# Strassen sums of the feed-forward's up weights with one operand copied into PSUM by ScalarE, and the eight gate rows two beside each of four column tiles

## The chip, the cores and the metric

The kernel runs on one NeuronCore of a Trainium2 chip. The metric is the device time of one launch in microseconds. The engines are named as the profile names them: PE is the matrix engine (its weight loads stand apart as PEld), DVE the vector engine, ACT the scalar engine, POOL GpSimd, SP the queue that issues all DMAs here. Each engine works through its instructions in the order in which they stand in the program; they wait for each other through semaphores.

## The reference, cut to what matters

One layer of a streaming encoder over 64 sample frames and 512 prompt frames, 576 columns in all, width 1024, all in float32. Attention, convolution and the first gate come first; the change lies in the second half:

```python
h2 = _rmsnorm(x, norm2_g) * (1 + sc2) + sh2
gate, up = jnp.split(h2 @ w_ffn_up, 2, axis=-1)      # w_ffn_up: 1024 x 5632, D_FF = 2816
x = x + gt2 * ((jax.nn.silu(gate) * up) @ w_ffn_down)  # w_ffn_down: 2816 x 1024
```

`gt2` is one of six vectors `silu(c) @ w_ada + b_ada`, one row of 1024 products for each of its 1024 elements and each of the two request groups.

## The kernel before

Activations lie transposed, 128 features on the partitions and tokens along the row. A weight tile is 128 by 128, a chunk is eight of them (512 KB), and every float32 product is made of three float32r matmuls: high part of the weights by high part of the activations, high by low, low by high (`mm3`, lines 323 to 325). So every chunk that arrives in a buffer `wraw` is split in units of four tiles: ACT casts the high part (`whi`, line 297), POOL or DVE subtracts it from the source (`wlo`, line 300). Four buffers of `whi` and four of `wlo` go round, five of `wraw`.

The feed-forward runs in three stretches of column tiles, `FCH`: pairs 0 to 7, 8 to 15, 16 to 21. A pair is one tile of gate columns and one of up columns; its two chunks are called g and u here. In each stretch `up(i)` makes every pair's activations, then `down` multiplies them by eight column tiles of `w_dn`. The up product of a pair is done by a 2 by 2 block scheme with seven products instead of eight, on half the tokens (288 columns) each, of 12 matmuls each. Product m takes as its weights: 1 and 2 the halves g0 and g1 of chunk g, 4 the half u1 of chunk u, and 5, 6, 7, 3 sums of the four halves. For pairs 0 to 7 the products 1 and 2 are made earlier. `pair_source` makes the sums:

```python
two = bank2(("cva", "sa")[n_sum[1] % 2])...      # a two-bank PSUM tile
sums[c, 5], sums[c, 6] = two[:, 0], two[:, 1]
nc.vector.tensor_add(out=sums[c, 5], in0=u0, in1=u1)            # line 270
nc.vector.tensor_sub(out=sums[c, 6], in0=sums[c, 5], in1=g0)    # line 271
```

The sums of one pair are made about one pair ahead of their use, into `cva` and `sa` in turn. Only the first pair's go elsewhere. Line 274 (POOL) makes the sum of product 7, line 277 (DVE) that of product 3.

The products of a pair accumulate in four PSUM banks. In `up`, product 5 goes to a bank `c5`, DVE reads it into `v` (line 1379), and only then may product 3 accumulate on the same bank; product 7 goes to `c7`, DVE adds it (line 1381), and only then may product 4 accumulate there. Line 1376 makes `u`, which 1379 and 1381 need ahead; lines 1383, 1387 and `act` (1372 to 1374) finish the pair.

Beside the first stretch's `down` the vector `gt2` is made, a column tile of it beside each of the eight column tiles of `w_dn`: `gate_row(n)` loads a chunk of `w_ada_n` into a buffer `wraw` (line 1245) and DVE multiplies it with two broadcast rows and sums (line 416, twice; the rows lie in `cva` and `sa`, where `gate_start` puts them). The following pairs' chunks use the same five buffers, and the following pairs' sums use the same two PSUM tiles.

A scheduler fixes each engine's order when the program is built, from the dependencies and its own times; the feed-forward isn't ordered by hand.

Of the kernel before, what the change touches and what calls it, by code (L numbers as in the profile page):

```python
# [87 lines left out]
def layer_kernel(ctx: ExitStack, tc: tile.TileContext, a):  # L88
    nc = tc.nc
# [4 lines left out]
    def sb(shape, tag, dt=F32, bufs=1):  # L94
        return cp.tile(shape, dt, tag=tag, name=tag, bufs=bufs)

    def bank(tag):
        return ps.tile([P, 512], F32, tag=tag, name=tag)

    def bank2(tag):  # L100
        return ps.tile([P, 2, 512], F32, tag=tag, name=tag)
# [83 lines left out]
    def vcol(o, i):  # L185
        return vec[:, o + i : o + i + 1]
# [65 lines left out]
    sums = {}  # L252

    def pair_source(c, m):

        if m in (1, 2):
            return raws[c - 1][:, 4 * m - 4 : 4 * m]
        if m == 4:
            return raws[c][:, 4:8]
        g0, g1, u0, u1 = (raws[c - 1 + x // 2][:, 4 * (x % 2) : 4 * (x % 2) + 4] for x in range(4))  # L260
        if m == 6:

            n_sum[1] += 1
            if n_sum[1] == 1:
                sums[c, 5] = pair_sum()
                sums[c, 6] = bank("m0").rearrange("p (k n) -> p k n", n=P)
            else:
                two = bank2(("cva", "sa")[n_sum[1] % 2]).rearrange("p x (k n) -> p x k n", n=P)
                sums[c, 5], sums[c, 6] = two[:, 0], two[:, 1]
            nc.vector.tensor_add(out=sums[c, 5], in0=u0, in1=u1)  # L270
            nc.vector.tensor_sub(out=sums[c, 6], in0=sums[c, 5], in1=g0)
        elif m == 7:
            sums[c, 7] = pair_sum()
            nc.gpsimd.tensor_sub(out=sums[c, 7], in0=g0, in1=u0)
        elif m == 3:
            sums[c, 3] = pair_sum()
            nc.vector.tensor_sub(out=sums[c, 3], in0=g1, in1=sums[c, 6])
        return sums[c, m]

    n_sum = [0, 0]  # L280

    def pair_sum():
        n_sum[0] += 1
        return ft([P, 4, P], f"wx{n_sum[0] % 2}")
# [44 lines left out]
    def mmbank():  # L329
        l = mmtags["l"]  # L330
        mmtags["i"] += 1
        return bank(l[mmtags["i"] % len(l)])
# [15 lines left out]
    with tc.tile_pool(name="sp", bufs=1) as sp:  # L348
# [153 lines left out]
        with tc.manual_schedule(engines={ENG.PE, ENG.DVE, ENG.Activation, ENG.Pool}):  # L502
            nc.scalar.activation(out=ct, in_=vec[:, V_CT : V_CT + 16].rearrange("p (k g) -> p k g", g=2), func=AF.Silu)
            nc.vector.scalar_tensor_tensor(
                out=bsn, in0=vec[:, V_BA + SC1 : V_BA + SC1 + 8], scalar=1.0, in1=vec[:, V_N1 : V_N1 + 8],
# [64 lines left out]
            for k in range(KT):  # L570
                n = k + 1
# [109 lines left out]
    def pool_tap(i, j):  # L681
# [24 lines left out]
        out=rbd.rearrange("h (q r) -> h q r", r=255),  # L706
        in_=rbs.unsqueeze(1).to_broadcast([16, 64, 255]),
# [18 lines left out]
    def products(kind, i, h):  # L726

        b = gemm(("in", N_IN.index((kind, i))), hx, (h,))[0]

        def out():  # L730
            if kind == "g":
                evac_g(h, b)
            elif kind == "a":
                evac_a(i, h, b)
            elif kind == "k":
                evac_k(i, h, b)
            elif kind == "v":
                evac_v(i, h, b)
            elif kind == "q":
                evac_q(i, h, b)  # L740
            else:
                j = i // 2 if kind == "ga" else gbs(i)
                if h == 0 and i % 2 == 0 and (kind == "ga" or i >= N_EARLY):
                    sigs[j] = sb([P, 2, NT], f"kv{j}")
                c0, c1 = HALF[h]
                o = sigs[j][:, i % 2, c0:c1] if j in sigs else None
                if kind == "gb" and i < N_EARLY:
                    if h == 0:
                        gbr[i] = sb([P, YW], f"gbr{i}") if i < 3 else at([P, NT], "sv")
                    nc.scalar.copy(out=gbr[i][:, c0:c1], in_=b)  # L750
                elif kind == "ga":
                    nc.scalar.copy(out=o, in_=b)
                else:
                    nc.scalar.activation(out=o, in_=b, func=AF.Sigmoid)

        return out
# [216 lines left out]
    with tc.manual_schedule(engines={ENG.PE, ENG.DVE, ENG.Activation, ENG.Pool}):  # L973
        for j, (p, ch, u) in enumerate(steps):
# [7 lines left out]
            out = products(*job[:2], *job[2]) if job else None  # L982
# [32 lines left out]
    with tc.tile_pool(name="lp", bufs=1) as lp:  # L1015
        def lt(shape, tag, dt=F32, bufs=1):
# [5 lines left out]
                            in_=cdram.rearrange("g d -> (g d)").partition_broadcast(P))  # L1022
# [5 lines left out]
        def wide(o):  # L1028
            return vec[:, o : o + 8].unsqueeze(2).to_broadcast([P, 8, 2])
# [110 lines left out]
    def ft(shape, tag, dt=F32, bufs=1):  # L1140
        if tag.startswith("gbr"):
            return sb(shape, tag, dt)
        return fp.tile(shape, dt, tag=tag, name=tag, bufs=bufs)
# [98 lines left out]
    def late_row(j, f, cbt):  # L1242

        t = sb([P, KT, P], "wraw", bufs=RAW).rearrange("p k n -> p (k n)")
        nc.sync.dma_start(out=t, in_=a["w_ada_n"][j])
        dump = sb([P, D], "lsum", BF16)
        ada_cols(ada[:, f], t, cbt, [dump, dump])

    for n in range(8):
# [7 lines left out]
        out=sc_a[:, 1], in0=ada[:, SC2 : SC2 + 8], scalar=1.0, in1=wide(V_N2), op0=ALU.add, op1=ALU.mult  # L1257
# [36 lines left out]
    with tc.manual_schedule(engines={ENG.PE}):  # L1294
# [8 lines left out]
        for j2 in (0, 2):  # L1303
# [6 lines left out]
            for j in t1:  # L1310
                nc.vector.scalar_tensor_tensor(
                    out=t1[j], in0=t1[j], scalar=sh2(j), in1=b0[:, j], op0=ALU.add, op1=ALU.subtract
                )
            for j in t1:
                nc.vector.scalar_tensor_tensor(
                    out=t2[j], in0=x11[:, j], scalar=sh2(4 + j), in1=t1[j], op0=ALU.add, op1=ALU.subtract
# [14 lines left out]
    def gate_start():  # L1331
        for g in range(2):
            cb3[g] = sb([P, KT, P], "wraw", bufs=RAW).rearrange("p k n -> p (k n)")
            nc.sync.dma_start(out=cb3[g], in_=cdram[g].partition_broadcast(P))
            to_psum(cb3, g, ("cva", "sa")[g])

    def gate_row(k):
        late_row(KT + len(ROW_SH) + 24 + k, GT2 + k, cb3)
        nc.vector.tensor_scalar_add(out=ada[:, GT2 + k], in0=ada[:, GT2 + k], scalar1=vcol(V_BA, GT2 + k))
# [63 lines left out]
    for c in range(len(FCH) - 1):  # L1403
        for i in range(*FCH[c]):
            up(i)
        mmtags["i"] = 3
        if c == 0:
            yt = [ft([P, 8, HB], "b0"), *(sb([P, 4, HB], f"kv{6 + x}") for x in range(2))]
            ysum = [[yt[0][:, n] for n in range(8)], [yt[1 + n // 4][:, n % 4] for n in range(8)]]
            gate_start()  # L1410
        for n in range(8):
            if c == 0:
                gate_row(n)
            for h in range(2):
                b = mmbank()[:, :HB]
                down(b, n, c, h)
                if c == 0:
                    nc.scalar.copy(out=ysum[h][n], in_=b)
                else:
                    nc.vector.tensor_add(out=ysum[h][n], in0=b, in1=ysum[h][n])  # L1420
                    residual(n, h, ysum[h][n], GT2)
    c = len(FCH) - 1
# [16 lines left out]
    for n in range(7):  # L1439
# [7 lines left out]
        if n == 1:  # L1447
            r = rst[0][2]()
            for k in range(8):
                nc.vector.scalar_tensor_tensor(  # L1450
                    out=x1[k][:, :HB], in0=x1[k][:, :HB], scalar=vcol(V_NF, k), in1=r, op0=ALU.mult, op1=ALU.mult,
# [5 lines left out]
    with tc.manual_schedule(engines={ENG.PE, ENG.DVE, ENG.Activation, ENG.Pool}):  # L1457
# [10 lines left out]
        for k in (0, 1, 2, 3, 4, 7):  # L1468
            nc.vector.scalar_tensor_tensor(
                out=y[:, k], in0=x1[k][:, HB:], scalar=vcol(V_NF, k), in1=r, op0=ALU.mult, op1=ALU.mult,  # L1470
# [119 lines left out]
```

## Time and profile before

| | us |
|---|---|
| median of three runs (948.9 to 953.95) | 952.08 |
| the profiled execution | 950.14 |
| its span, first to last instruction | 948.4 |
| PE busy in the span | 915.4 |
| DVE busy | 689.8 |
| ACT busy | 465.6 |
| POOL busy | 530.5 |

The profile is of one execution. Times of rows count from the start of its span; 1.74 us lie outside it. The feed-forward's up stretches lie at about 557 to 626 us, 678 to 767 us and 829 to 897 us of the span, its down stretches between and after them.

### The profile page before, as it was taken

How to read it: one execution, taken by the hardware profiler on the slowest of the kernel's cores; microseconds unless marked ns; L12 is line 12 of the kernel's file. 1: busy time of each engine (PE TensorE's matmuls, PEld its weight loads, DVE VectorE, ACT ScalarE, POOL GpSimd, SP SyncE). 2: the span in 40 equal slices, each digit the busy share in tenths (PEclk: the TensorE clock that was granted, in tenths of full speed). 3: DMA queues.
4: the chain of work that ended last, by engine and by line, in shares of the span. 5: the costliest groups of instructions: out<-in, count | busy, mean ns of one | idle time of the engine just before them, and what ended most of it. 6: DMA issues, size and time to landing. Idle time of an engine off the chain costs nothing.

```text
span 948.4 us, 18132 instructions
## 1 busy us (share of the span) xinstructions
PE 915.4 (97%) x6804; PEld 901.8 (95%) x6804; DVE 689.8 (73%) x1372; ACT 465.6 (49%) x1055; POOL 530.5 (56%) x495
## 2 busy tenths in 40 slices
PE   7989999999999999999999999999999999999995
PEld 4989999999999999999999989999899999999995
DVE  6988999868888884589967698844566644556475
ACT  5436555466555566552434764453254541255462
POOL 2759999445454546453573565654367664376322
PEclk8999999999999999999999999999999999999997
DMA  9914423222122123286463244355322232222352
GB/s 338 360 55 53 150 77 100 68 84 68 45 68 68 46 95 106 84 305 224 180 241 112 67 134 134 112 156 198 136 90 90 89 112 72 67 96 88 88 149 100
DMA packets 37918, 116.33 MB, mean 123 GB/s; under 512 B 4243, under 2 KB 9011, under 8 KB 37685
## 3 DMA queue, kind: packets, MB, share of 16 engines
q1 hardware_dynamic: 37830, 115.18, 37.0%
q8 instruction: 53, 0.87, 0.4%
q14 instruction: 35, 0.29, 0.1%
HBM read 111.11 MB, written 4.18 MB: 122 GB/s over the span
## 4 chain that ended last, share of the span: by engine, by line
PE 66%; DVE 16%; DMA 10%; issue 4%; ACT 1%; POOL 1%; SPq 0%; DVEq 0%; ACTq 0%; POOLq 0%
PE m L323 12%; PE m L324 11%; PE m L325 11%; PE s L323 8%; PE s L325 8%; PE s L324 8%; DVE dump L416 5%; DMA wraw<-w_ada_n 3%; DMA wraw<-w_up 3%; DVE lsum L416 2%; DMA wat<-w_ada_n 2%; PE sa L923 1%; DVE h L481 1%; DVE qa L439 1%; DVE wlo L300 1%
## 5 line engine op out<-in xcount | busy, mean ns | idle before, releaser
L300 POOL TENSOR_TENSOR wlo<-wraw,whi 128x512 fp32r<-128x512 f32 x216 | 291.8, 1359 | 217.2 <-ACT whi L297 173.6
L297 ACT CAST whi<-wraw 128x512 fp32r<-128x512 f32 x248 | 149.5, 608 | 162.3 <-PE s L324 86.3
L323 PE MATMUL m<-h,whi 128*128 128x320 f32 (+2 forms) x768 | 227.0, 296 | 2.1 <-ACT whi L297 2.1
L324 PE MATMUL m<-h,whi 128*128 128x320 f32 (+2 forms) x768 | 225.8, 295 | 0.0
L325 PE MATMUL m<-h,wlo 128*128 128x256 f32 (+2 forms) x768 | 225.0, 295 | 0.2 <-DVE wlo L300 0.2
L323 PEld LDWEIGHTS m<-h,whi 128*128 128x128 f32 x768 | 145.1, 189 | 2.8 <-ACT whi L297 2.6
L325 PEld LDWEIGHTS m<-h,wlo 128*128 128x128 f32 x768 | 144.6, 189 | 0.4 <-DVE wlo L300 0.4
L324 PEld LDWEIGHTS m<-h,whi 128*128 128x128 f32 x768 | 144.8, 189 | 0.0
L671 DVE SCALAR_TENSOR_TENSOR cva<-z,vec,cva 128x606 f32<-128x606 f32 x150 | 127.5, 850 | 1.5
L323 PE MATMUL s<-h,whi 128*128 128x288 f32 (+2 forms) x336 | 99.4, 296 | 2.2 <-ACT kv L1287 1.9
L325 PE MATMUL s<-h,wlo 128*128 128x288 f32 (+2 forms) x336 | 98.9, 294 | 0.0
L324 PE MATMUL s<-h,whi 128*128 128x288 f32 (+2 forms) x336 | 98.8, 294 | 0.0
L300 POOL TENSOR_TENSOR wlo<-wx,whi 128x512 fp32r<-128x512 f32 x44 | 56.7, 1291 | 58.3 <-ACT whi L297 52.8
L324 PE MATMUL m<-qa,whi 128*128 128x288 f32 (+2 forms) x272 | 80.3, 295 | 0.0
L323 PE MATMUL m<-qa,whi 128*128 128x288 f32 (+2 forms) x272 | 80.2, 296 | 0.0
L325 PE MATMUL m<-qa,wlo 128*128 128x288 f32 (+2 forms) x272 | 79.9, 294 | 0.0
L323 PE MATMUL s<-qa,whi 128*128 128x288 f32 (+2 forms) x240 | 70.9, 296 | 0.0
L324 PE MATMUL s<-qa,whi 128*128 128x288 f32 (+2 forms) x240 | 70.9, 295 | 0.0
L325 PE MATMUL s<-qa,wlo 128*128 128x288 f32 (+2 forms) x240 | 70.4, 295 | 0.2 <-DVE wlo L300 0.2
L323 PE MATMUL s<-kv,whi 128*128 128x288 f32 x216 | 64.7, 300 | 4.5 <-DVE t L1379 3.5
L323 PEld LDWEIGHTS s<-h,whi 128*128 128x128 f32 x336 | 63.5, 189 | 2.8 <-ACT kv L1287 2.1
L324 PE MATMUL s<-kv,whi 128*128 128x288 f32 x216 | 63.9, 296 | 0.0
(421 smaller groups left out, 2332.5 us busy)
## 6 DMA issues: line engine op xcount, KB each, us to landing
wraw<-w_up SPq DMA_DIRECT2D x52, 512.0 KB, 3.3
wraw<-w_in SPq DMA_DIRECT2D x39, 512.0 KB, 3.4
wat<-w_ada_n SPq DMA_DIRECT2D x16, 512.0 KB, 3.5
wraw<-w_ada_n SPq DMA_DIRECT2D x16, 512.0 KB, 4.1
wraw<-w_dn SPq DMA_DIRECT2D x16, 512.0 KB, 3.5
wraw<-w_dn SPq DMA_DIRECT2D x16, 384.0 KB, 3.1
wraw<-w_ao SPq DMA_DIRECT2D x8, 512.0 KB, 3.4
wraw<-w_co SPq DMA_DIRECT2D x8, 512.0 KB, 4.2
```

The source lines that it names most:

```text
L297: nc.scalar.copy(out=hi, in_=src)
L300: eng.tensor_sub(out=lo, in0=src, in1=hi.bitcast(F32))
L323: nc.tensor.matmul(out, lhsT=hi, rhs=xh, start=first, stop=False, skip_group_check=again)
L324: nc.tensor.matmul(out, lhsT=hi, rhs=xl, start=False, stop=False, skip_group_check=again)
L325: nc.tensor.matmul(out, lhsT=lo, rhs=xh, start=False, stop=last, skip_group_check=again)
L416: nc.vector.scalar_tensor_tensor(out=dumps[g], in0=wt, scalar=1.0, in1=cbt[g], op0=ALU.mult, op1=ALU.mult, accum_out=out[:, g : g + 1],)
L439: nc.vector.scalar_tensor_tensor(out=xt[k][:, s0:s1], in0=xt[k][:, s0:s1], scalar=sc_a[:, 0, k, g : g + 1], in1=rstd[:, s0:s1], op0=ALU.mu ...
L481: nc.vector.scalar_tensor_tensor(out=hl[k][:, s0:s1], in0=xt[k][:, s0:s1], scalar=ada[:, f, g : g + 1], in1=hh[k][:, s0:s1].bitcast(F32), ...
L671: nc.vector.scalar_tensor_tensor(out=acc, in0=src, scalar=w, in1=acc, op0=ALU.mult, op1=ALU.add)
L923: nc.tensor.transpose(pts[0][:, j, u], probs[u][:, j].rearrange("p a b -> p (a b)"), ident)
```

## The change

Two edits. In `pair_source`, ACT copies u0 into the PSUM tile and DVE adds u1 to it there, where DVE added u0 and u1 out of SBUF; the first pair's sum is left as it was. In the first stretch's `down`, column tiles 0 to 3 have two gate rows each, and 4 to 7 none.

```diff
                 two = bank2(("cva", "sa")[n_sum[1] % 2]).rearrange("p x (k n) -> p x k n", n=P)
                 sums[c, 5], sums[c, 6] = two[:, 0], two[:, 1]
-            nc.vector.tensor_add(out=sums[c, 5], in0=u0, in1=u1)
+                nc.scalar.copy(out=sums[c, 5], in_=u0)
+            nc.vector.tensor_add(out=sums[c, 5], in0=sums[c, 5] if n_sum[1] > 1 else u0, in1=u1)
             nc.vector.tensor_sub(out=sums[c, 6], in0=sums[c, 5], in1=g0)
...
         for n in range(8):
-            if c == 0:
-                gate_row(n)
+            if c == 0 and n < 4:
+                gate_row(2 * n)
+                gate_row(2 * n + 1)
             for h in range(2):
```

Lines 270 to 1412 of before stand one line lower in the changed file, those after the second edit two; the new copy is line 270 there, the add 271.

The scheduler also moves instructions. In the second stretch's up pairs, DVE before, where `t<-m` is line 1376, `cva<-wraw` the add, `t<-s` first line 1379 and then 1381:

```order
L1376 TENSOR_TENSOR t<-m_8598,t 128x288
L270 TENSOR_TENSOR cva<-wraw 128x512
L1379 TENSOR_TENSOR t<-s_8599,t 128x288
L271 TENSOR_TENSOR cva<-cva,wraw 128x512
L1381 TENSOR_TENSOR t<-s_8600,t 128x288
L300 TENSOR_TENSOR wlo<-sa,whi 128x512
```

The same place now:

```order
L1377 TENSOR_TENSOR t<-m_8607,t 128x288
L1380 TENSOR_TENSOR t<-s_8608,t 128x288
L271 TENSOR_TENSOR cva<-cva,wraw 128x512
L272 TENSOR_TENSOR cva<-cva,wraw 128x512
L1382 TENSOR_TENSOR t<-s_8609,t 128x288
L301 TENSOR_TENSOR wlo<-sa,whi 128x512
```

The read of product 5 (now line 1380) stands ahead of the add, and the add and the subtraction stand together ahead of the read of product 7 (now 1382). It is so in all pairs of the second and third stretch that make a sum, but for the first of each. On ACT the new copy stands there between two casts of weights, as the third row of this piece of the changed program shows (`m` and `s` are banks of products, `wx` a sum of weights):

```order
L1361 COPY t<-m_8612 128x288
L1374 CAST qa_8518<-s_8462 128x288
L298 CAST whi<-wx_8666 128x512
L298 CAST whi<-wraw 128x512
L270 COPY cva<-wraw 128x512
L298 CAST whi<-wraw 128x512
L1364 ACTIVATE t<-m_8612 128x288
L298 CAST whi<-sa 128x512
```

Behind it stand the next pair's first cast, the silu of product 2 and the cast of the next pair's product 6.

In the first stretch's up pairs the third one's DVE rows before, from the add on (`t<-m` is 1379, then 1381):

```order
L270 TENSOR_TENSOR sa<-wraw 128x512
L1379 TENSOR_TENSOR t<-m_7254,kv_6637 128x288
L300 TENSOR_TENSOR wlo<-cva,whi 128x512
L271 TENSOR_TENSOR sa<-sa,wraw 128x512
L1374 TENSOR_TENSOR qa_7059<-s_7148,qa_7058 128x288
L1381 TENSOR_TENSOR t<-m_7255,t 128x288
```

And now:

```order
L271 TENSOR_TENSOR sa<-sa,wraw 128x512
L1380 TENSOR_TENSOR t<-m_7256,kv_6637 128x288
L301 TENSOR_TENSOR wlo<-cva,whi 128x512
L272 TENSOR_TENSOR sa<-sa,wraw 128x512
L1375 TENSOR_TENSOR qa_7059<-s_7149,qa_7058 128x288
L1382 TENSOR_TENSOR t<-m_7257,t 128x288
```

Here the add stays ahead of the read of product 5, in this pair and in the fifth; in the fourth and the sixth the read comes first.

In the first `down`, SP's queue before, from the two broadcast rows (`cdram`) on; `w_dn` are the down weights, `w_ada_n` the gate rows, `w_up` the next pairs' chunks:

```order
L1334 DMA wraw<-cdram 128x1024 x2
L1245 DMA wraw<-w_ada_n 128x1024
L248 DMA wraw<-w_dn 128x1024
L1245 DMA wraw<-w_ada_n 128x1024
L248 DMA wraw<-w_dn 128x1024
L1245 DMA wraw<-w_ada_n 128x1024
L248 DMA wraw<-w_dn 128x1024
L1245 DMA wraw<-w_ada_n 128x1024
L248 DMA wraw<-w_up 128x1024
L1245 DMA wraw<-w_ada_n 128x1024
L248 DMA wraw<-w_up 128x1024
L1245 DMA wraw<-w_ada_n 128x1024
```

And now:

```order
L1335 DMA wraw<-cdram 128x1024 x2
L1246 DMA wraw<-w_ada_n 128x1024 x2
L248 DMA wraw<-w_dn 128x1024
L1246 DMA wraw<-w_ada_n 128x1024 x2
L248 DMA wraw<-w_dn 128x1024
L1246 DMA wraw<-w_ada_n 128x1024 x2
L248 DMA wraw<-w_dn 128x1024
L1246 DMA wraw<-w_ada_n 128x1024 x2
L248 DMA wraw<-w_up 128x1024 x16
```

All eight gate rows stand ahead of the first chunk of the next pairs, where four of them stood between and behind those chunks. On ACT the copies of pairs 8 and 9 now stand among the casts of the last down chunk, ahead of that chunk's first and second half.

## Rows read from the trace of the kernel before

**Rows 1.** The page's first part: busy time of each engine.
```profile
PE 915.4 (97%) x6804; PEld 901.8 (95%) x6804; DVE 689.8 (73%) x1372; ACT 465.6 (49%) x1055; POOL 530.5 (56%) x495
```

**Rows 2.** PE's waits, 557 to 625 us: who waited for whom, us, times, longest.
```profile
PE m L323 <- DVE t L1379: 1.0, 1, 1.0
PE s L323 <- ACT qa L1373: 0.9, 1, 0.9
PE m L323 <- ACT qa L1373: 0.9, 1, 0.9
PE s L323 <- DVE t L1379: 0.5, 1, 0.5
PE m L323 <- ACT whi L297: 0.4, 1, 0.4
```

**Rows 3.** PE's waits, 690 to 900 us.
```profile
PE s L323 <- DVE t L1379: 3.0, 5, 0.9
```

**Rows 4.** PE's waits, 625 to 690 us.
```profile
PE m L323 <- ACT whi L297: 1.7, 1, 1.7
```

**Rows 5.** Groups by line and shape, from 500 us: busy, mean ns, idle before.
```profile
L270 DVE TENSOR_TENSOR cva<-wraw 128x512 f32<-128x512 f32 x11 | 13.4, 1219 | 15.2 <-DMA wraw<-w_up 15.2
...
L270 DVE TENSOR_TENSOR sa<-wraw 128x512 f32<-128x512 f32 x10 | 11.8, 1180 | 13.2 <-DMA wraw<-w_up 13.2
...
L271 DVE TENSOR_TENSOR cva<-cva,wraw 128x512 f32<-128x512 f32 x11 | 7.5, 686 | 0.0
```

**Rows 6.** Timeline of DVE in the second stretch: start, length, in brackets idle before.
```profile
734.97 1.78 DVE L270 TENSOR_TENSOR sa<-wraw 128x512 f32<-128x512 f32 x1 [2.40 <-DMA wraw<-w_up]
736.67 0.44 DVE L1379 TENSOR_TENSOR t<-s,t 128x288 f32<-128x288 f32 x1
```

**Rows 7.** Timeline of PE at that place and in the first `down`.
```profile
673.69 0.29 PE L323 MATMUL s<-qa,whi 128*128 128x288 f32 x1
...
736.11 0.29 PE L325 MATMUL s<-kv,wlo 128*128 128x288 f32 x1
737.26 0.37 PE L323 MATMUL s<-kv,whi 128*128 128x288 f32 x1 [0.85 <-DVE t L1379]
737.47 0.29 PE L324 MATMUL s<-kv,whi 128*128 128x288 f32 x1
...
738.93 0.29 PE L323 MATMUL m<-h,whi 128*128 128x288 f32 x1
```

**Rows 8.** Timeline of DVE in the third stretch, where PE does not wait.
```profile
843.71 0.71 DVE L270 TENSOR_TENSOR cva<-wraw 128x512 f32<-128x512 f32 x1 [2.37 <-DMA wraw<-w_up]
```

**Rows 9.** Timeline of ACT: a copy of 1024 columns into PSUM, three casts.
```profile
635.53 1.02 ACT L172 COPY sa<-wraw 128x1024 f32<-128x1024 f32 x1 [3.44 <-DMA wraw<-cdram]
636.48 0.62 ACT L297 CAST whi<-wraw 128x512 fp32r<-128x512 f32 x1
...
665.84 0.62 ACT L297 CAST whi<-wraw 128x512 fp32r<-128x512 f32 x1 [0.98 <-PE s L324]
...
735.03 0.62 ACT L297 CAST whi<-wraw 128x512 fp32r<-128x512 f32 x1 [1.23 <-PE m L324]
```

**Rows 10.** Timeline of DVE in the first stretch, the third pair.
```profile
579.36 1.56 DVE L270 TENSOR_TENSOR sa<-wraw 128x512 f32<-128x512 f32 x1 [0.49 <-DMA wraw<-w_up]
580.83 0.44 DVE L1379 TENSOR_TENSOR t<-m,kv 128x288 f32<-128x288 f32 x1
```

**Rows 11.** Line 416 from 625 us on: shortest, median, longest ns, first and last start.
```profile
L416 DVE SCALAR_TENSOR_TENSOR lsum<-wraw,cva x8: 1207/1222/1222, 636.8 to 676.2; 128x1024 bf16<-128x1024 f32 x8
```

**Rows 12.** Timeline of DVE after the last gate row.
```profile
678.58 0.70 DVE L270 TENSOR_TENSOR cva<-wraw 128x512 f32<-128x512 f32 x1
```

**Rows 13.** Busy time and instructions by stretch: PE, PEld, DVE, ACT, POOL, clock, DMA.
```profile
679.90:686.05 6.15, 4.23 (x19) 3.77 (x18) 3.73 (x7) 3.12 (x6) 3.39 (x3) 0.72 0.25 84
686.05:692.20 6.15, 6.15 (x49) 6.15 (x48) 2.92 (x5) 2.14 (x4) 4.72 (x4) 1.00 0.40 131
```

**Rows 14.** The page's DMA issues: number, KB each, us to landing.
```profile
wraw<-w_up SPq DMA_DIRECT2D x52, 512.0 KB, 3.3
```

## The prediction

> **What bounds the kernel now.** I read the page's first part first: PE is busy for 915.4 us of the 948.4 us span, no other engine for more than 73% [rows 1]. The change neither adds nor removes a matmul, so whatever it gives or takes comes out of PE's idle time and of stretches at the lower clock. PE's waits by stretch come next. In the first up stretch there are two of 0.9 us on ACT's `qa` (line 1373), one of 1.0 and one of 0.5 on DVE's line 1379, and one of 0.4 on a cast [rows 2]. In the second and third stretch five add up to 3.0 us, all on line 1379 [rows 3]. Where the first `down` passes into pair 8 there is one of 1.7 us on a cast [rows 4]. These are all that the change can reach.
>
> Why line 1379 is late is in DVE's timeline: line 270 waits 2.40 us for a chunk of `w_up`, starts at 734.97, takes 1.78 us, and 1379, queued behind it, starts at 736.67, though it needs nothing of that chunk [rows 6]. PE had started the last matmul of the products ahead at 736.11 and stood 0.85 us until 1379 was through [rows 7]. The eleven sums into `cva` alone waited 15.2 us for their chunks [rows 5].
>
> **What a wait costs.** From 736.11 to the second matmul behind the wait, 737.47, are 1.36 us; two steps at 0.126 us (6.15 us for 49 matmuls, [rows 13]) would take 0.25, so 1.11 is lost against 0.85 of idle time. I add 0.26 to every wait.
>
> **The copy and the add: durations.** A copy by ACT of 1024 columns into PSUM takes 1.02 us, a cast of 512 columns 0.62 [rows 9]. The new copy of 512 columns lies between half of the one, 0.51, and the other, 0.62; I take 0.6, nearer to the row of equal width. 21 copies are 12.6 us on an engine busy for 465.6 us [rows 1].
>
> The add now has one operand in PSUM. The nearest row is line 271, the same operation in that form: 686 ns on the mean of eleven, against 1219 for line 270 [rows 5]. So DVE should spare 0.5 us a time, 11 us in all, nearly none of it on the path. Line 270 is not always long: 0.71 us at 843.71 [rows 8] and 0.70 at 678.58 [rows 12], 1.78 at 734.97 [rows 6]; in the trace it is long where POOL works beside it. The Trainium skill has a rule for this ("SBUF — State Buffer", section Who interferes with whom): a DVE instruction with two inputs in SBUF contends with a GpSimd instruction that reads SBUF, one with a single such input doesn't. Line 271's even 686 ns agree with it, and by it the add takes that time everywhere. If instead the chunk just landed made the operation slow, the add would stay at up to 1.78 us; the shortened waits below would then not shrink, 0.5 us less in the sum. I take 0.69.
>
> **A: the second and third stretch.** There line 1379 (now 1380) stands ahead of the add, and at once follows 1376, long before product 3 needs it. All five waits go: 3.0 + 5 x 0.26 = 4.3 us. What is late next is the read of product 7, line 1381 (now 1382), which now stands behind add and subtraction. For the pair of [rows 6]: landing 734.97, copy 0.6, add 0.69, subtraction 0.69, the read itself 0.44 (as line 1379), end at 737.39. Product 4 starts four matmuls behind 738.93 [rows 7], at 739.43 by the step above; without the wait 1.11 earlier, 738.32. Some 0.9 us of slack, so no new wait. On ACT the copy delays the cast of 735.03 to 735.57, and it is over at 736.2; its weights are used at 738.93 - 1.11 = 737.8 [rows 7, 9]. The silu and the cast of product 6 behind move by about 0.5 us and are due later still. The add is in PSUM, so the chunk's buffer comes free as before: its last reader is a later split or sum, and the transfers keep their distance from PE.
>
> **B: the first stretch.** The two waits of 0.9 stand on ACT's cast `qa`, line 1373, which reads what DVE's line 1372 leaves; I take them for the fourth and sixth pair, where 1372, like 1379, stood behind line 270. Now both come ahead of the add there: 1.8 + 2 x 0.26 = 2.3 us go. In the third and fifth the add stays ahead of the read: before, 1.56 us from 579.36 and 1379 at 580.83 [rows 10]; now copy and add, 0.6 + 0.69 = 1.29, so 0.27 earlier, twice, 0.5 us. The 0.4 us on a cast stays [rows 2]. Together 2.8.
>
> **C: the gate rows.** Before, each row's chunk reuses the buffer of the row ahead: a transfer (3.3 us for such a size, [rows 14]) and two of line 416 (1.22 each) make some 5.8, and the starts measured, 636.8 to 676.2 for eight, are 5.63 apart [rows 11]. The sums of pairs 8 and 9 stand behind the last on DVE, the first at 678.58 [rows 12]; PE, done with `down`, waits 1.7 us [rows 4], and the granted clock of the next 6.15 us is 0.72: a part of them at 1.2 GHz, 19 matmuls against 49 in the 6.15 us behind [rows 13]. Lost: 30 x 0.126 = 3.8 us.
>
> Now two chains run beside each other, four rows long. A round takes at least 5.63, and at most one transfer and four of line 416, 3.3 + 4.9 = 8.2, so the last row ends between 636.8 + 3 x 5.63 + 4.9 = 658.6 and 666.3; I take 662, between them. The pairs' chunks, queued behind on SP, land up to two transfers later: 669, at worst 673. The sums need them by 678.5, so the wait goes and the clock stays up, 3.8 us. What could be late in its place are the casts of the last down chunk, before which the two copies now stand on ACT: the last of these casts ran at 665.84 [rows 9], PE used it at 673.69 [rows 7], and it now comes at 669 + 0.6, hidden by 3 us; at the worst, 673 + 1.2, PE waits a half us there. The down chunk that now queues behind the second row on SP starts 2 to 3 us later, with several column tiles before it is due.
>
> **The sum.** 4.3 + 2.8 + 3.8 = 10.9 us; 950.14 - 10.9 = 939.2 for an execution like the profiled one. That one lies 1.94 below the median of the three runs, so on the median 952.08 - 10.9 = 941.2, which is my number; 939.2 belongs in the range. If smaller gaps of PE beside the listed waits go too, which the rows do not list, the low end is lower; I put it at 937, two us under 939.2.
>
> **The rivals.** (i) *The transition keeps its wait*: the pairs' chunks come as late as before, since SP works in order and a split of `down` holds a buffer. Against it speak the 12 us between 666.3 and 678.5. It gives 941.2 + 3.8 = 945.0. Chance 0.12.
>
> (ii) *The wait moves on*: product 4 waits for 1382 in place of product 3, or ACT's queue, stopped by the copy, delays a cast. For it speaks that ACT did stop 3.44 us for a transfer with a cast behind it [rows 9]. The Trainium skill ("PSUM — Partial Sum Buffer", section Engine vs sequencer instructions) says that ScalarE's queue is strictly first in, first out; by that alone every us that a chunk lands later holds the casts behind the copy as long, and the trace's cast at 636.48 agrees. Half of A and B lost: 941.2 + 3.6 = 944.8. Chance 0.13.
>
> (iii) *No change*: both of these together, because the chunks land late throughout: 10.9 - 3.8 - 3.6 = 3.5 us left, 948.6, which lies within 0.5% (4.8 us). Chance 0.12.
>
> (iv) *Slower*: the order add, subtraction, 1382 makes product 4 wait in every steady pair. Slack is 0.9 us; beyond it each us of landing costs PE one us in some 13 pairs. To lose the 10.9 and 4.8 more, 15.7 / 13 = 1.2 us a pair: decided at landings 2.1 us later than now, out of a transfer of 3.3 [rows 14]. It would need transfers to start later, and nothing in the change holds a buffer longer but the copy's 0.6. It gives 957 or more. Chance 0.08.
>
> **How the numbers follow.** The forecast has 0.55: 937 to 942.5, the costs' bounds and the 1.94 among it. To hold 8 in 10 the range takes in (i) and (ii), 937 to 947. What a measurement can tell from no change is about 0.5%, 4.8 us; faster by more is the forecast with (i) and (ii), 0.80; within it 0.12; slower 0.08.
>
> **What would show it.** In the profile after: lines 271 and 272 both at 0.69 us, the copy at 0.5 to 0.62; no wait of PE on 1380 in the second and third stretch, none on 1382; two short ones left in the first; the last gate row before 667, no wait of PE at the start of pair 8 and a granted clock of 1.00 there. The forecast is wrong if PE waits for 1382 or a `whi` cast in most pairs, if the copies wait longer than DVE's sums did, or if the clock falls anywhere in `down`.

## The result

The changed kernel takes 937.61 us (median of six runs, 935.88 to 938.70), the kernel before 953.02 in its six (947.32 to 956.32): a ratio of 0.985, interval 0.9827 to 0.9873. The forecast was 941.2 with a range of 937 to 947, and faster with a chance of 0.80. In later comparisons the kernel before has medians of 949.86 (23 runs), 950.13 and 948.44 (11 each); against these the gain is 11 to 12.5 us.

The profiled execution of the changed kernel takes 935.88 us, its span is 934.1 against 948.4. The page of it, against [rows 1]:

```profile
PE 909.1 (97%) x6804; PEld 898.9 (96%) x6804; DVE 678.0 (73%) x1372; ACT 476.2 (51%) x1076; POOL 526.1 (56%) x495
```

DVE lost 11.8 us, ACT gained 10.6, POOL lost 4.4. Where the 14.3 us of span are is seen when the start of each matmul, counted from the start of the span, is compared in the two traces:

| part of the program | forecast, us | gained, us |
|---|---|---|
| up to 555 us (557 in the trace before), the same instructions in the same order | 0 | 2.0 |
| B, first up stretch | 2.8 | 3.6 |
| C, passage into pair 8 | 3.8 | 3.9 |
| A, second and third stretch | 4.3 | 4.8 |
| the rest | 0 | 0.0 |

So the change is worth 12.3 us between these two executions, and 2.0 are what executions differ by ahead of it. (The expectations below take 3.5, 4.0 and 4.7 for B, C and A, a tenth off each.) Of the 2.0, 1.0 is one wait that the list in [rows 2] leaves out: PE waited 1.9 us for a copy by ACT (line 1287) just ahead of 557 us in the kernel before, and waits 0.9 us for it now. The first pair's sums, which the change leaves as they were, stand ahead of that copy; their add took 1.78 us in that execution and takes 0.69 in this one.

PE's waits after, 557 to 625 us, against [rows 2] (who waited for whom, us, times, longest); the second stands in the second pair, where the wait of 0.4 us on a cast was:

```profile
PE m L324 <- DVE t L1380: 0.4, 1, 0.4
PE s L324 <- DVE t L1380: 0.2, 1, 0.2
```

From 625 to 690 us there is none, where [rows 4] had 1.7 (and one of 0.2 on a split, not listed there), and from 690 to 900 only this one, on a split, where [rows 3] had 3.0 on the read of product 5:

```profile
PE s L326 <- DVE wlo L301: 0.2, 1, 0.2
```

The sums' groups from 500 us on, against [rows 5] (busy, mean ns, idle before and for whom):

```profile
L271 DVE TENSOR_TENSOR cva<-cva,wraw 128x512 f32<-128x512 f32 x11 | 7.7, 698 | 16.6 <-ACT cva L270 16.5
L272 DVE TENSOR_TENSOR cva<-cva,wraw 128x512 f32<-128x512 f32 x11 | 7.6, 695 | 0.2
...
L270 ACT COPY cva<-wraw 128x512 f32<-128x512 f32 x11 | 6.5, 591 | 11.5 <-DMA wraw<-w_up 11.5
```

Add and subtraction take 0.70 us each, the copy 0.59, in every pair. DVE's wait for the chunk has become one for ACT's copy, about as long (16.6 us against 15.2 for `cva`); what changed is what stands behind it. DVE in a pair of the second stretch:

```profile
722.34 0.46 DVE L1380 TENSOR_TENSOR t<-s,t 128x288 f32<-128x288 f32 x1 [0.91 <-PE s L326]
724.49 0.70 DVE L271 TENSOR_TENSOR sa<-sa,wraw 128x512 f32<-128x512 f32 x1 [1.69 <-ACT sa L270]
725.23 0.70 DVE L272 TENSOR_TENSOR sa<-sa,wraw 128x512 f32<-128x512 f32 x1
725.84 0.45 DVE L1382 TENSOR_TENSOR t<-s,t 128x288 f32<-128x288 f32 x1
```

ACT there, the copy and the cast that it stands ahead of:

```profile
723.87 0.59 ACT L270 COPY sa<-wraw 128x512 f32<-128x512 f32 x1 [0.99 <-DMA wraw<-w_up]
724.40 0.62 ACT L298 CAST whi<-wraw 128x512 fp32r<-128x512 f32 x1
```

And PE's first matmul of product 4 in this pair:

```profile
727.44 0.29 PE L324 MATMUL s<-kv,whi 128*128 128x288 f32 x1
```

The read of product 5 is over at 722.80, long before the add. The read of product 7, behind the subtraction, ends at 726.29, 1.15 us ahead of its use.

At the passage, the gate rows' first multiplication (shortest, median, longest ns, first and last start), against [rows 11]:

```profile
L417 DVE SCALAR_TENSOR_TENSOR lsum<-wraw,cva x8: 1208/1221/1222, 631.0 to 656.1; 128x1024 bf16<-128x1024 f32 x8
```

The two copies for pairs 8 and 9 on ACT:

```profile
659.12 0.59 ACT L270 COPY sa<-wraw 128x512 f32<-128x512 f32 x1 [4.36 <-DMA wraw<-w_up]
...
665.15 0.59 ACT L270 COPY cva<-wraw 128x512 f32<-128x512 f32 x1 [4.59 <-DMA wraw<-w_up]
```

And the stretch that answers to the first of [rows 13] (the columns after the length are PE, PEld, DVE, ACT and POOL busy, each with its count, the granted clock and DMA):

```profile
672.45:678.60 6.15, 6.15 (x49) 6.15 (x48) 1.74 (x3) 3.24 (x7) 4.19 (x4) 1.00 0.29 85
```

Rows that took 39 us from first to last start take 25 [rows 11]; the clock stays at 1.00, and PE runs 49 matmuls where it ran 19.

### The profile page after: what moved, and what is told of

The parts are those of the page before. It is cut to its first block, busy times and chain, and to the rows that moved or that the text cites. A ratio compares the mean times of both kernels' runs of the same rounds, so it can differ in the third digit from the quotient of the medians.

```text
span 934.1 us, 18156 instructions
## 1 busy us (share of the span) xinstructions
PE 909.1 (97%) x6804; PEld 898.9 (96%) x6804; DVE 678.0 (73%) x1372; ACT 476.2 (51%) x1076; POOL 526.1 (56%) x495
## 4 chain that ended last, share of the span: by engine, by line
PE 75%; DVE 15%; DMA 5%; issue 2%; ACT 2%; POOL 1%; SPq 0%; DVEq 0%; ACTq 0%; POOLq 0%
PE m L324 13%; PE m L326 13%; PE m L325 13%; PE s L324 10%; PE s L325 9%; PE s L326 9%; DVE dump L417 6%; DMA wat<-w_ada_n 2%; DMA wraw<-w_ada_n 2%; DVE lsum L417 1%; PE sa L924 1%; DVE qa L440 1%; DVE h L482 1%; DMA wraw<-w_up 1%; DVE z L1080 1%
## 5 line engine op out<-in xcount | busy, mean ns | idle before, releaser
L301 POOL TENSOR_TENSOR wlo<-wraw,whi 128x512 fp32r<-128x512 f32 x216 | 287.7, 1341 | 210.0 <-ACT whi L298 167.7
```

The lines of the kernel that those rows point to most:

```text
L301: eng.tensor_sub(out=lo, in0=src, in1=hi.bitcast(F32))
```

## The experiments

The theory: the first edit works by the place of the read of product 5 in DVE's queue, the second by the end of the last gate row. The rivals: the add's length does it; the gate rows' spacing does it; ACT's queue is close to being the next bound. Nine more kernels were timed against the kernel before; ratios are to it. Diffs are against the changed kernel unless a sentence says otherwise.

**The copy alone.** The gate rows stand as before.

```diff
-            if c == 0 and n < 4:
-                gate_row(2 * n)
-                gate_row(2 * n + 1)
+            if c == 0:
+                gate_row(n)
```

> The copy as changed, the gate rows one beside each column tile as before. By the two traces the up stretches gave 3.5 and 4.7 us and the passage into pair 8 gave 4.0. Theory (the two edits act in different places and add up): 8.2 us come, PE waits 1.7 us at the passage and the granted clock falls there as in [rows 13]; ratio to the kernel before about 0.991, or 0.989 with the 2 us by which the two executions differ ahead of the change. Rival (the gate rows, done earlier, also bring the later chunks earlier, and part of the gain in the second stretch is theirs): waits on line 1380 or 1382 remain in the second stretch, less than 6 us, ratio above 0.993.

Measured: 939.72 us, ratio 0.9895 (0.987 to 0.992). The waits of the second and third stretch are gone, and at the passage stands, of PE's waits from 625 to 690 us:

```profile
PE m L324 <- ACT whi L298: 2.0, 1, 2.0
```

The theory holds: the copy brings what it brings without the gate rows. One part of the expectation failed: the granted clock did not fall behind the wait, it is 1.00 there. So, matmul by matmul, this execution loses 2.7 us to the changed one at the passage, less than the 3.9 of the kernel before, though the wait is longer; that is taken up at the end.

**The gate rows alone.** Here the diff is against the kernel before.

```diff
-            if c == 0:
-                gate_row(n)
+            if c == 0 and n < 4:
+                gate_row(2 * n)
+                gate_row(2 * n + 1)
```

> The gate rows as changed, the sums as before: DVE adds u0 and u1 out of SBUF. Theory: 4.0 us come at the passage, its wait and the lower clock are gone, and the waits on line 1379 stay, about 4 to 5 us of them in the second and third stretch; ratio about 0.996. Rival (the copy is what lets pair 8's sums be ready): the passage keeps its wait, ratio 0.999 or more.

Measured: 946.74 us, ratio 0.9972 (0.9955 to 0.9988). PE's wait on a cast at the passage is gone and the clock stays up; a wait of 0.4 us on a POOL split is there instead. The passage gains 3.1 us on the kernel before, 3.7 without that split. In all the last matmul starts 5.3 us earlier, 1.2 of it ahead of the change; the first stretch is 1.1 shorter, though its instructions and their order are those of the kernel before, because the add of the sixth pair took 0.70 us here and 1.63 there, and the wait behind it is not there. The second stretch is 1.3 longer by 713 us, with longer waits. The waits on line 1379 stay, six of them from 557 to 900 us in this form:

```profile
PE s L323 <- DVE t L1379: 4.5, 6, 0.8
```

The two ratios multiply to 0.9867, beside the 0.985 of both together, whose interval holds it. The edits add up, as far as these intervals can tell; by the traces the second edit is worth 2.7 to 3.9 us, depending on the execution.

**The copy into SBUF.** ACT's copy goes to a tile in SBUF, so the add reads two operands there. DVE's order is that of the changed kernel, and ACT's too, but for the first copy, which stands further ahead and starts 4 us earlier.

```diff
-                nc.scalar.copy(out=sums[c, 5], in_=u0)
-            nc.vector.tensor_add(out=sums[c, 5], in0=sums[c, 5] if n_sum[1] > 1 else u0, in1=u1)
+                u0c = sb([P, 4, P], "lsum")
+                nc.scalar.copy(out=u0c, in_=u0)
+            nc.vector.tensor_add(out=sums[c, 5], in0=u0c if n_sum[1] > 1 else u0, in1=u1)
```

> As the changed kernel, but ACT copies u0 into a tile in SBUF, so that the add has two operands in SBUF again; the order on DVE and ACT is the changed kernel's, row for row. Theory (in the second and third stretch the place of the add in DVE's queue decides, not its length): the add takes 1.2 to 1.8 us where POOL works beside it, line 1382 comes up to 1.1 us later, within the 1.2 us that it has, and no wait appears there; only the first stretch's third and fifth pair, where the add stands ahead of line 1380, lose 0.5 to 1.1 each: 1 to 2 us slower than the changed kernel, ratio about 0.987. Rival (the shorter add is what took the waits away): most of the 8.2 us are lost, ratio about 0.993. A second one (the add was long because its chunk had just landed, whatever POOL does): it is long in every pair, also where POOL stands.

Measured: 940.02 us, ratio 0.9891 (0.9869 to 0.9912); the trace is 2.8 us longer than the changed kernel's, 2.1 of it by the end of the first `down`, 0.7 behind. PE's waits on the read of product 5 (line 1381 here) from 690 to 900 us:

```profile
PE s L325 <- DVE t L1381: 0.5, 1, 0.5
```

The five of the kernel before are gone. The one here is in the third stretch's first pair, where PE hardly waited before, and where the add stands ahead of the read (it starts at 821.59, the read at 823.04). In the steady pairs the add is long and nothing waits. DVE in one of them:

```profile
737.82 1.21 DVE L272 TENSOR_TENSOR cva<-lsum,wraw 128x512 f32<-128x512 f32 x1 [1.76 <-ACT lsum L271]
739.07 0.70 DVE L273 TENSOR_TENSOR cva<-cva,wraw 128x512 f32<-128x512 f32 x1
739.68 0.45 DVE L1383 TENSOR_TENSOR t<-s,t 128x288 f32<-128x288 f32 x1
```

The read of product 7 ends at 740.13, product 4 starts at 740.70. So the place decides there; the length decides only where the add stands first: in the first stretch, where PE waits 2.3 us on the read here against 0.6 in the changed kernel, and in the pair just named. The loss in the trace is somewhat over the 1 to 2 us expected.

This kernel also shows what makes the add long. POOL, and below it DVE, in the first stretch:

```profile
577.02 1.30 POOL L302 TENSOR_TENSOR wlo<-wraw,whi 128x512 fp32r<-128x512 f32 x1
```

```profile
570.87 0.70 DVE L272 TENSOR_TENSOR cva<-lsum,wraw 128x512 f32<-128x512 f32 x1 [0.64 <-ACT lsum L271]
...
577.83 1.05 DVE L272 TENSOR_TENSOR sa<-lsum,wraw 128x512 f32<-128x512 f32 x1 [1.01 <-ACT lsum L271]
```

POOL's operation ends at 578.32 and the add 0.56 us later, at 578.88. At 570.87 POOL stands and the add takes 0.70, though the copy ahead of it had just waited for the chunk; [rows 8] has such a short add right behind a landing in the kernel before. Of the 21 adds those that began while POOL worked end about 0.55 us behind POOL's operation, where that is later than 0.70 us after their own start; all others take 0.70. The second rival falls. The Trainium skill says it so ("SBUF — State Buffer", section Who interferes with whom): a DVE operation with two inputs in SBUF contends with a GpSimd operation that reads SBUF, and the one issued first blocks the other for its whole length. The rows agree in who waits for whom; held up for the whole length, the add would end 0.7 us behind POOL's operation, and it ends 0.55 to 0.57 behind.

**The order without the copy.** The diff is against the kernel with the gate rows alone: DVE adds out of SBUF, ACT copies nothing, but the add is queued behind the read of product 5.

```diff
-            nc.vector.tensor_add(out=sums[c, 5], in0=u0, in1=u1)
+            if v_ins[0] is None:
+                nc.vector.tensor_add(out=sums[c, 5], in0=u0, in1=u1)
+            else:
+                with tc.issue_after(v_ins[0]):
+                    nc.vector.tensor_add(out=sums[c, 5], in0=u0, in1=u1)
...
+    v_ins = [None]
...
-        nc.vector.tensor_add(out=v, in0=c5, in1=u)
+        v_ins[0] = nc.vector.tensor_add(out=v, in0=c5, in1=u).ins
```

> The gate rows as changed, the sums as before without a copy by ACT (DVE adds u0 and u1 out of SBUF), but in every pair the add is queued on DVE behind the read of product 5, which the scheduler did not do by itself. Theory (the gain of the second and third stretch comes from that place in the queue; the copy is only what made the scheduler put it there): no wait of PE on line 1379 in any stretch, the add still up to 1.8 us long beside POOL, product 4 not waiting, since the landing is followed by 1.78 + 0.69 + 0.44 = 2.9 us where the changed kernel has 2.4 and 1.2 to spare: as fast as the changed kernel or a us faster for the first stretch, ratio 0.984 to 0.986. Rival (the copy itself, by a short add, is needed): waits on line 1381 come up in most pairs of these stretches, 0.5 us each, ratio above 0.989.

Measured: 937.77 us, ratio 0.9885 (0.986 to 0.991). From 690 to 900 us PE waits for no read at all, only for the same split as in the changed kernel:

```profile
PE s L330 <- DVE wlo L305: 0.2, 1, 0.2
```

DVE in a steady pair; the add out of SBUF takes 1.20 us and delays nobody (product 4 starts at 707.32):

```profile
704.07 0.46 DVE L1384 TENSOR_TENSOR t<-s,t 128x288 f32<-128x288 f32 x1 [2.71 <-PE s L330]
704.45 1.20 DVE L274 TENSOR_TENSOR cva<-wraw 128x512 f32<-128x512 f32 x1
705.68 0.70 DVE L275 TENSOR_TENSOR cva<-cva,wraw 128x512 f32<-128x512 f32 x1
706.28 0.45 DVE L1386 TENSOR_TENSOR t<-s,t 128x288 f32<-128x288 f32 x1
```

Behind 619 us this trace and the changed kernel's stay within 0.2 us of each other. The whole of A comes without a copy: the copy did nothing there but lead the scheduler to the other order. At the last matmul this trace is 2.5 us behind the changed kernel's, 1.8 of it ahead of the first sum and 0.6 in the first stretch, where the long adds make PE wait twice for the read of product 7, 0.3 and 0.2 us. The ratio was missed: 0.9885 lies above the 0.984 to 0.986 expected and below the rival's 0.989, and its interval holds both; its median in us is that of the changed kernel (937.77 and 937.61), and the kernel before was faster in this comparison. It is the trace that decides: the rival's waits on the read of product 7 in most pairs are not in it.

**The gate rows late.**

```diff
-            if c == 0 and n < 4:
-                gate_row(2 * n)
-                gate_row(2 * n + 1)
+            if c == 0 and n >= 4:
+                gate_row(2 * n - 8)
+                gate_row(2 * n - 7)
```

> As the changed kernel, but the eight gate rows lie two beside each of column tiles 4 to 7. Theory (what decides is when the last row is done, since the sums of pair 8 stand behind it on DVE): the rows take some 27.5 us from first to last, as in the changed kernel, begin about 643, and end about 672 to 676, when PE needs the sums: the wait and the lower clock are back, 3 to 8 us slower than the changed kernel, ratio 0.988 to 0.993. Rival (two chains beside each other are enough wherever they stand): as the changed kernel, 0.985.

Measured: 951.29 us, ratio 1.0019 (1.0002 to 1.0036). All of the gain is gone, that of the copy too; I had the direction and missed the size, 14 us against 3 to 8. PE's wait at the passage:

```profile
PE m L324 <- ACT whi L298: 12.3, 1, 12.3
```

ACT's copy for pair 8 waits for the tile `cva`, which holds a broadcast row until the last gate row has read it:

```profile
683.90 0.59 ACT L270 COPY cva<-wraw 128x512 f32<-128x512 f32 x1 [7.18 <-DVE lsum L417]
```

The stretch behind the wait:

```profile
688.53:694.68 6.15, 6.15 (x31) 6.13 (x32) 2.42 (x4) 2.23 (x5) 5.09 (x4) 0.64 0.29 85
```

The rows began at 648.13 and took 36.9 us to their end, 685.04, not 27.5. In this kernel the next pairs' chunks stand between them on SP's queue and hold buffers; the last two rows started at 676.75 and 682.63, 5.88 apart, as rows do that share one buffer [rows 11]. I had taken the changed kernel's duration without asking which buffers are left. What the experiment says stands: the end of the last row decides.

**The gate rows early.**

```diff
-            if c == 0 and n < 4:
-                gate_row(2 * n)
-                gate_row(2 * n + 1)
+            if c == 0 and n < 2:
+                for j in range(4):
+                    gate_row(4 * n + j)
```

> As the changed kernel, but the eight gate rows lie four beside each of column tiles 0 and 1. Theory (only the end of the last row counts, and it has 14 us to spare in the changed kernel): no gain and no loss, ratio 0.985 as the changed kernel, last row at or before 659. Rival (the down chunks, which now queue behind four and eight rows on SP, come late): PE waits for casts in the first `down`, over 1 us, ratio 0.987 or more.

Measured: 937.06 us, ratio 0.9855 (0.983 to 0.9879); no wait of PE in `down` or at the passage. The last row's first multiplication starts at 652.0, 4 us before the changed kernel's, and that is worth nothing:

```profile
L417 DVE SCALAR_TENSOR_TENSOR lsum<-wraw,cva x8: 1207/1216/1221, 630.7 to 652.0; 128x1024 bf16<-128x1024 f32 x8
```

**Four copies for one.**

```diff
+                for x in (u1, u0, u1):
+                    nc.scalar.copy(out=sums[c, 5], in_=x)
                 nc.scalar.copy(out=sums[c, 5], in_=u0)
```

> As the changed kernel, with three more copies of the same size ahead of each copy on ACT, 63 in all, 37 us of ACT by 0.59 each; the scheduler knows of them and puts the add behind the read of product 7 in most pairs. Theory (ACT, busy for half of the span, has the room, and the casts behind the copies have 2 us or more before their use): no wait of PE on lines 1380 or 1382 in the second and third stretch, at most a few tenths on casts, not more than 3 us slower than the changed kernel, ratio 0.985 to 0.988. Rival (ACT's queue is the next bound, as in case (ii) of the prediction): PE waits for `whi` casts in most pairs, 0.5 us or more each, 10 us slower, ratio 0.995 or more.

Measured: 937.61 us, ratio 0.9866 (0.9842 to 0.989); at the end of the first stretch the trace is 2.4 us behind the changed kernel's, 0.8 of it there before the first sum and 1.6 in the first stretch; the whole span is 1.6 us longer. ACT is busy for 507.6 us. From 690 to 900 us PE waits 0.2 us, on the same split; the two waits that came are in the first stretch:

```profile
PE m L328 <- DVE wlo L303: 0.9, 1, 0.9
PE m L326 <- DVE qa L1377: 0.6, 1, 0.6
```

In the steady pairs ACT's queue is far from being the next bound; in the first stretch the longer queue does cost. How late the copy may come before product 4 waits was not measured by this: the scheduler, which knows of the copies, puts the add behind the read of product 7.

**The first pair too.** The changed kernel leaves the first pair's subtraction with two operands in SBUF. Here ACT copies one of them to PSUM first.

```diff
+            if n_sum[1] == 1:
+                nc.scalar.copy(out=sums[c, 6], in_=g0)
-            nc.vector.tensor_sub(out=sums[c, 6], in0=sums[c, 5], in1=g0)
+            nc.vector.tensor_sub(out=sums[c, 6], in0=sums[c, 5], in1=sums[c, 6] if n_sum[1] == 1 else g0)
```

> As the changed kernel, and for the first pair ACT copies g0 into the PSUM tile first, so that the subtraction has one operand in SBUF and one in PSUM. In the changed kernel it has two in SBUF, takes 1.78 us at 550.76 with POOL beside it, ACT waits 2.17 us for it and PE 0.93 us at 555.01 for a copy behind that wait. Theory (two operands in SBUF beside POOL make the operation long): 0.69 us, ACT's wait is a us shorter, PE's wait at the beginning of the first up stretch is under 0.2 us, 0.8 to 1.2 us faster than the changed kernel: ratio 0.984, which only the trace can tell from 0.985. Rival (it is long for another reason, or PE's wait has another cause): the operation stays over 1.2 us or the wait stays at 0.9.

Measured: 935.13 us (934.10 to 935.87), ratio 0.9841 (0.9814 to 0.9868). The subtraction in the changed kernel, and here:

```profile
550.76 1.78 DVE L272 TENSOR_TENSOR m<-wx,wraw 128x512 f32<-128x512 f32 x1
```

```profile
550.66 0.68 DVE L274 TENSOR_TENSOR m<-wx,m 128x512 f32<-128x512 f32 x1
```

PE's wait from 540 to 557 us, in the changed kernel as below, is gone, and the trace gains 1.1 us at that place:

```profile
PE s L324 <- ACT kv L1288: 0.9, 1, 0.9
```

It has the lowest median of the study; the trace tells it from the changed kernel, the ratios don't.

**The first pair too, with the add behind the read everywhere.** The diff is against the kernel ahead of this one.

```diff
-            nc.vector.tensor_add(out=sums[c, 5], in0=sums[c, 5] if n_sum[1] > 1 else u0, in1=u1)
+            if v_ins[0] is None:
+                nc.vector.tensor_add(out=sums[c, 5], in0=sums[c, 5] if n_sum[1] > 1 else u0, in1=u1)
+            else:
+                with tc.issue_after(v_ins[0]):
+                    nc.vector.tensor_add(out=sums[c, 5], in0=sums[c, 5] if n_sum[1] > 1 else u0, in1=u1)
...
+    v_ins = [None]
...
-        nc.vector.tensor_add(out=v, in0=c5, in1=u)
+        v_ins[0] = nc.vector.tensor_add(out=v, in0=c5, in1=u).ins
```

> As the changed kernel, with the first pair's subtraction out of PSUM as in first_too, and the add queued behind the read of product 5 in every pair. Theory: the two waits on line 1382 that are left in the first stretch of first_too (0.3 and 0.2 us, each with 0.26 more) go too, 1 us faster than first_too, ratio 0.983 to 0.984; no wait of PE over 0.2 us between 540 and 860 us. Rival (behind that read the sums come late for product 6 of the next pair): new waits on `whi` casts in the first stretch, no gain over first_too.

Measured: 935.35 us, ratio 0.9854 (0.9832 to 0.9877). The two waits on the read are gone, but another came, on the cast of product 6, and the rest of the first stretch loses small steps:

```profile
PE s L331 <- ACT whi L305: 0.5, 1, 0.5
```

No gain over the kernel ahead of it: my expectation was wrong, the rival right. In the first stretch the sums are needed sooner, and neither order is free there.

## Why the prediction was right

**What bounds the kernel.** Right. Nearly all that was gained behind the first sums lies at the waits listed in [rows 2 to 4] and at the lower clock of [rows 13]. The longest wait of the first stretch, 1.9 us on line 1287, is not in [rows 2]; the change does not touch what stands ahead of it, and the 1.0 us that came there was not the change's.

**A.** Five waits were to go, 4.3 us; they went and gave 4.2, and 0.6 more came from two small steps that the list of waits leaves out. The reason given was right, and stronger than I put it: with the same order and a long add (the copy into SBUF) or no copy at all, the gain is there. The next in line, the read of product 7, has 1.15 us to spare in the pair shown, where I had 0.9.

**B.** Forecast 2.8, measured 3.6. The two waits behind line 1372 gave 2.2, where I had 2.3, and a new step of 0.35 came at 585 us. Of the 0.4 on a cast, counted as staying, 0.3 went. The two shortened waits gave 1.3, where I had 0.5: this term was mis-sized, for a different reason in each pair. In the third pair, copy and add brought the read 0.23 us nearer the landing, as computed; 0.35 more came because the chunk landed earlier against PE's work. That is luck: three other kernels have the same order up to the gate rows (copy alone, rows late, rows early), and PE's wait in the third pair is 0.2, 0.8 and 0.9 us in them, against 0.4 here. In the fifth pair the wait is gone in all four. I had let the add follow the landing there too, but before the change it did not wait for the chunk, only for DVE's own work ahead of it; the copy now runs for the most part beside that work, so the 1.07 us by which the add is shorter counted, and not the difference to copy and add. The add in the fifth pair, before and after:

```profile
596.94 1.77 DVE L270 TENSOR_TENSOR sa<-wraw 128x512 f32<-128x512 f32 x1
```

```profile
593.50 0.70 DVE L271 TENSOR_TENSOR sa<-sa,wraw 128x512 f32<-128x512 f32 x1 [0.45 <-ACT sa L270]
```

With the copy into SBUF, where the add is long again, that pair's wait is back with 0.5 us. Nor is the sixth pair's wait, half of the 2.2, there in every execution of the old order: the kernel with the gate rows alone did not have it.

**C.** Forecast 3.8, measured 3.9. The last row ended at 658.53 and pair 9's copy ran at 665.15. The trace is 5.6 us ahead of the one before at that place, so on the times of the prediction these are 664.1, between 658.6 and 666.3 where I took 662, and 670.8, where I had 669. That the size came out so well is in part luck: the loss was counted in the same execution that it was then compared with, and with the copy alone, where the clock did not fall, the passage costs 2.7.

**Durations.** Copy 0.59 (0.6 taken), add 0.70 (0.69). The doubt about the add, whether POOL or the landed chunk makes it long, is settled for POOL.

**The total.** 10.9 us were forecast and 12.3 measured in the traces. The rest of the 15.4 us between the medians is, as far as the traces show, no part of the change: 2.0 us lie ahead of it, and the kernel before has lower medians in the later comparisons. The measured median is 3.6 us under my number and only 0.6 above the low end of the range. I had put that end two us lower for small gaps of PE; what filled most of it was the 2.0 us ahead of the change, so that the range held is in part luck, while the three mechanisms are right. What makes the runs of the kernel before scatter over 9 us, where the changed kernel's six lie within 3, is open; two steps of 1 us each that come and go between its executions are shown in the last section.

**The rivals.** (i) and (ii) did not come. (ii) would have needed ACT's queue to be tight, and four copies for one cost 1.6 us, none of it in the steady pairs of the second and third stretch. (iii) and (iv) are out by the ratio; the point from which (iv) decides was not reached by any run.

## What to carry to other kernels

A wait is paid by what stands behind it in the queue: look first at whether an instruction that waits for a transfer stands ahead of one that doesn't need it, and move that one, before making the waiting one shorter. Where a scheduler fixes the order, an edit to an operand also changes the order, so compare the orders and test the order by itself; here it was the whole gain of two stretches. Chains that recycle one buffer are judged by the end of their last link against the moment when something needs it; two chains side by side help only until that moment is met, and not where other transfers take the second buffer.

## What the runs showed of the hardware

A wait of PE of nearly the same length cost the clock in one execution and not in another, at the same place of the program. In the kernel before, PE was idle for 1.7 us [rows 4], and this is the stretch behind the wait:

```profile
681.93:683.93 2.00, 1.80 (x7) 1.57 (x8) 1.29 (x3) 1.86 (x4) 1.34 (x2) 0.64 0.00 0
683.93:685.93 2.00, 2.00 (x10) 2.00 (x9) 1.12 (x3) 0.62 (x1) 1.92 (x2) 0.51 0.10 16
```

With the copy alone PE was idle for 2.0 us, and the same stretch reads:

```profile
676.90:678.90 2.00, 1.80 (x11) 1.57 (x12) 1.29 (x3) 1.86 (x4) 1.35 (x2) 1.00 0.00 0
678.90:680.90 2.00, 2.00 (x17) 2.00 (x16) 1.03 (x3) 0.62 (x1) 1.92 (x2) 1.00 0.20 31
```

The clock stands in the third place from the end, 1.00 for 2.4 GHz. The first ran in part at 1.2 GHz, the second at 2.4 throughout, 17 matmuls in 2 us against 10. And a wait seven times as long, in the kernel with late gate rows, brought the clock of the 6.15 us behind it to 0.64, hardly lower than the 0.72 that the 6.15 us from 681.93 have here. So the idle time of a wait and what it costs in clock are to be counted apart, and the second can differ from run to run.

Which of the two is lengthened, an add with two operands in SBUF or the POOL operation that meets it, can turn on tenths of a microsecond between executions, and in the two cases seen here it was worth 1 us each. The sixth pair's add and POOL's operation, in the kernel before and in the kernel with the gate rows alone, whose order is the same there:

```profile
605.57 1.29 POOL L300 TENSOR_TENSOR wlo<-wraw,whi 128x512 fp32r<-128x512 f32 x1
```

```profile
605.79 1.63 DVE L270 TENSOR_TENSOR cva<-wraw 128x512 f32<-128x512 f32 x1 [0.72 <-DMA wraw<-w_up]
```

```profile
604.36 0.70 DVE L270 TENSOR_TENSOR cva<-wraw 128x512 f32<-128x512 f32 x1 [0.48 <-DMA wraw<-w_up]
```

```profile
604.40 1.81 POOL L300 TENSOR_TENSOR wlo<-wraw,whi 128x512 fp32r<-128x512 f32 x1
```

Where POOL began first the add took 1.63 us and PE waited 0.9 behind it; where the add began 0.04 us ahead of POOL, POOL's operation took 1.81 and PE did not wait. The first pair's add is a second case: 1.78 us in the kernel before, 0.69 after the change, with 1.0 us more of waiting at line 1287. With the gate rows alone it takes 0.68 and POOL's operation 1.87, though POOL's begins 0.04 us ahead in the records; so close together they don't tell which came first. Without the SBUF operands of the sums POOL is busy 4.4 us less, though it does the same work.
